# A sink logit kept as a 257th score column, and rotated queries in a shared scratch tile, in a two-layer decoder trunk

## The chip, the core and the metric

The kernel runs on one core of one Trainium2 chip. The metric is the device time of one execution in microseconds (us). Five instruction streams run side by side and meet through semaphores: PE (TensorE, matrix products; PEld is its weight load), DVE (VectorE), ACT (ScalarE), POOL (GpSimd) and SP (SyncE, which here only issues transfers). Each stream is executed strictly in its own order: an instruction that has to wait holds up everything behind it on its engine.

## The reference, cut to what matters

The program computes a two-layer decoder on 512 tokens of width 1024, in float32. The change touches the attention of layer 0: eight query heads in two groups that share one key and one value head each, a causal window of 128 tokens, and a learned logit per head (the sink) that enters the softmax's maximum and its denominator but has no value vector.

```python
def band_attention(q, k, v, max_dist, sink=None):
    s = jnp.einsum('bnqhgd,bnjhd->bnhgqj', qb, kk) * (hd ** -0.5)
    s = jnp.where(valid[None, :, None, None], s, -jnp.inf)
    m = jnp.max(s, axis=-1)
    m = jnp.maximum(m, sink_b)
    p = jnp.exp(s - m[..., None])
    l = jnp.sum(p, axis=-1)
    l = l + jnp.exp(sink_b - m)
    o = jnp.einsum('bnhgqj,bnjhd->bnqhgd', p.astype(v.dtype), vv)
    o = o / jnp.transpose(l, (0, 1, 4, 2, 3))[..., None]
    ...

def even_mixer(h, w_in, sinks, conv_w, conv_b, ln_g, ln_b, w_out, pos):
    proj = jnp.einsum('bsd,de->bse', h, w_in)
    q, k, v, glu = jnp.split(proj, [A_Q, A_Q + A_KV, A_Q + 2 * A_KV], axis=-1)
    q = rotary(q.reshape(B, S, A_HEADS, HEAD_DIM), pos)
    ...
    a, _ = band_attention(q, k, v, A_WINDOW - 1, sinks)
    c = g_a * jax.nn.sigmoid(g_b)
    c = causal_depthwise_conv(c, conv_w, conv_b)          # 31 taps
    c = jax.nn.silu(layer_norm(c, ln_g, ln_b))
    return jnp.einsum('bse,ed->bsd', jnp.concatenate([a, c], axis=-1), w_out)
```

After this mixer come a feed-forward block, a second mixer, a second feed-forward block and a last norm; none of their code changes.

## The kernel before, in words

Activations lie transposed, features on the 128 partitions and the 512 tokens along the row. Every large product is done as three matmuls, since both sides are split into a rounded part and its remainder: weights come from memory as 128x1024 blocks (`raw`), ACT makes the rounded half `w_hi` (L174), and DVE or POOL subtracts to make `w_lo` (L151). One 128x128 weight tile costs three matmuls of 512 columns (L201, L202, L203).

Layer 0's mixer runs, by the span of the profile, from about 25 us to about 200 us. PE's order there is written by hand: the string `C0["steps"]` lists the projections (`g0` to `g3` of the convolution's gate pairs, `v`, `k`, `q0` to `q3`) and the attention steps (`S0` to `S3` scores, `V0` to `V3` values, each for one pair of heads i and i + 4; "head 0" to "head 3" below are these pairs), and a class `Seq` weaves the small attention steps between the projections' weight tiles. On the other engines a scheduler sets the order when the program is built, from the dependencies, from priorities and from its own estimate of durations; so a change of one instruction there can move others.

What DVE does in this stage: the rotation of queries and keys (`rope`, L390 to L393), the split of the rotated queries (`qs`, L717), the masked minimum of the negated scores (L598, one per block of 128 queries and head: it writes the negated scaled scores to `Pm` and their row minimum with the negated sink to `nm`), the sink's terms (`es`, L605; `rl`, L614 and L615), the product with the reciprocal denominators that ends the values of a head pair (`on`, L430), and most taps of the convolution, each one instruction on 128x512 (L481 and L483, which adds into a bank of PSUM, and L484, which adds that to POOL's part `yc`). The convolution runs at a much lower priority (`LATER`). ACT does the exponentials (L610) with their row sums `l`, the sink's exponential (L612), the copies of transposed probabilities `pts` (L410), which PE's value products (L421) wait for, the copy `oh` (L363) of a finished head pair, and products `prod` (L478) of some taps, which POOL adds up (L479). `prod` has three buffers, so a fourth product waits for POOL's first add. POOL also makes `w_lo` here.

PE has two kinds of meeting point with this: L435 transposes `on`, so it waits for DVE's L430, and L407 transposes the probabilities `Pm` for the next head pair into a bank that ACT's L644 (`yn`, the convolution's transposed output) may still read.

## Time and profile before

| what | value |
|---|---|
| time of three runs | 1117.32, 1123.54, 1124.16 us; median 1123.54 us |
| the profiled execution | 1121.61 us, of which the span from first to last instruction is 1119.9 us |
| PE busy | 1071.8 us (96% of the span) |
| DVE busy | 693.8 us (62%) |
| ACT busy | 572.9 us (51%) |
| POOL busy | 232.8 us (21%) |
| granted TensorE clock, mean | 0.989 |

The shares are means over the whole span. The page's table of 40 slices (28 us each) shows that they hide a stage: DVE's digits are 9, 7 and 7 in slices 3 to 5 (56 to 140 us: 7, 7, 4 for ACT, 7, 5, 4 for POOL), and PE, which has 9 nearly everywhere, has 8 or 7 only in some places, of which slices 3 and 5 are two. Rows of the timeline give the start, the duration, engine, line, operation, what is written and read, how many instructions of a kind in a row, and in brackets the idle time ahead and what ended it.

### The profile page before, as it was taken

What the parts mean: (1) busy time and instruction counts of PE and PEld (TensorE: products, weight loads), DVE (VectorE), ACT (ScalarE), POOL (GpSimd) and SP (SyncE); (2) the same over time, 40 slices, a digit from 0 to 9 for tenths busy, and PEclk for the clock granted to TensorE, in tenths of its full rate; (3) what the DMA queues carried; (4) which work ended last, traced back from release to release, by engine and by line L of the source; (5) the groups of instructions that cost most, each with busy time, mean ns of one, the idle gap of its engine ahead of it and who ended that gap; (6) DMA issues with size and microseconds to landing.
All of it is one profiled execution on the core that took longest, in us unless ns stands there. A gap on an engine that the chain in (4) does not pass through costs nothing.

```text
span 1119.9 us, 13693 instructions
## 1 busy us (share of the span) xinstructions
PE 1071.8 (96%) x5118; PEld 887.8 (79%) x5118; DVE 693.8 (62%) x1059; ACT 572.9 (51%) x930; POOL 232.8 (21%) x210
## 2 busy tenths in 40 slices
PE   9988789989999999999999999999899999999997
PEld 7767677868788888888887888888688888888785
DVE  3889965777455655654748546666765646555543
ACT  6577756754435343543636654446544453535433
POOL 0789754201101010100014300001111010101002
PEclk9989999999999999999999999999999999999999
DMA  6221112977767677621432111239777676767122
GB/s 230 68 70 57 38 38 75 263 208 190 168 187 150 188 136 217 135 57 50 149 103 76 57 39 58 94 117 237 210 187 179 164 171 180 154 189 150 26 69 76
DMA packets 42803, 145.89 MB, mean 130 GB/s; under 512 B 4848, under 2 KB 5744, under 8 KB 42736
## 3 DMA queue, kind: packets, MB, share of 16 engines
q1 hardware_dynamic: 31072, 102.97, 27.0%
q0 software_dynamic: 11520, 41.95, 22.2%
q8 instruction: 40, 0.66, 0.2%
q14 instruction: 27, 0.22, 0.1%
q10 hardware_dynamic: 144, 0.09, 0.0%
HBM read 142.89 MB, written 2.10 MB: 129 GB/s over the span
## 4 chain that ended last, share of the span: by engine, by line
PE 75%; DVE 9%; DMA 4%; ACT 4%; issue 4%; POOL 3%; POOLq 0%; ACTq 0%; SPq 0%; DVEq 0%
PE bank L201 11%; PE bank L202 10%; PE bank L203 10%; PE bank L904 10%; PE bank L907 10%; PE bank L906 10%; DMA raw<-in_ws 4%; PE bank L262 2%; PE bank L264 2%; PE bank L263 2%; DVE bank L483 2%; PE bank L919 1%; PE bank L421 1%; ACT w2h L880 1%; POOL yc L479 1%
## 5 line engine op out<-in xcount | busy, mean ns | idle before, releaser
L151 DVE TENSOR_TENSOR w2l<-raw,w2h 128x1024 fp32r<-128x1024 f32 x140 | 171.4, 1225 | 206.0 <-ACT w2h L880 206.0
L880 ACT ACTIVATE w2h<-raw 128x1024 fp32r<-128x1024 f32 x140 | 148.0, 1058 | 208.8 <-PE bank L907 159.5
L174 ACT ACTIVATE w_hi<-raw 128x512 fp32r<-128x512 f32 x204 | 127.4, 628 | 180.5 <-PE bank L202 143.4
L870 POOL DMA_DIRECT2D raw<-in_ws x80 | 69.6, 870 | 557.7 <-DVE w2l L151 231.7
L151 DVE TENSOR_TENSOR w_lo<-raw,w_hi 128x512 fp32r<-128x512 f32 x164 | 115.6, 709 | 57.7 <-ACT w_hi L174 57.7
L907 PE MATMUL bank<-w2h,s 128*128 128x512 f32 x320 | 126.0, 394 | 4.3 <-DVE s L151 4.3
L904 PE MATMUL bank<-w2h,s 128*128 128x512 f32 x320 | 126.5, 395 | 2.5 <-ACT s L823 1.4
L906 PE MATMUL bank<-w2l,s 128*128 128x512 f32 x320 | 125.5, 392 | 0.0
L201 PE MATMUL bank<-xh,w_hi 128*128 128x512 f32 x272 | 111.4, 410 | 1.3 <-ACT w_hi L174 1.3
L203 PE MATMUL bank<-xh,w_lo 128*128 128x512 f32 x272 | 108.0, 397 | 0.0
L202 PE MATMUL bank<-xl,w_hi 128*128 128x512 f32 x272 | 107.9, 397 | 0.0
L201 PE MATMUL bank<-hh,w_hi 128*128 128x512 f32 x256 | 100.1, 391 | 1.1 <-DVE hl L151 1.1
L202 PE MATMUL bank<-hl,w_hi 128*128 128x512 f32 x256 | 100.0, 391 | 0.0
L203 PE MATMUL bank<-hh,w_lo 128*128 128x512 f32 x256 | 99.9, 390 | 0.0
L904 PE MATMUL bank<-w2h,xh 128*128 128x512 f32 x240 | 94.4, 393 | 0.0
L907 PE MATMUL bank<-w2h,xl 128*128 128x512 f32 x240 | 93.5, 389 | 0.0
L906 PE MATMUL bank<-w2l,xh 128*128 128x512 f32 x240 | 93.4, 389 | 0.0
L907 PEld LDWEIGHTS bank<-w2h,s 128*128 128x128 f32 x320 | 60.7, 190 | 17.9 <-DVE s L151 5.2
L904 PEld LDWEIGHTS bank<-w2h,s 128*128 128x128 f32 x320 | 60.6, 190 | 16.4 <-ACT s L823 2.3
L906 PEld LDWEIGHTS bank<-w2l,s 128*128 128x128 f32 x320 | 60.5, 189 | 12.4
L151 POOL TENSOR_TENSOR w_lo<-raw,w_hi 128x512 fp32r<-128x512 f32 x40 | 54.6, 1366 | 60.2 <-ACT w_hi L174 57.6
L479 POOL TENSOR_TENSOR yc<-yc,prod 128x512 f32<-128x512 f32 x44 | 60.7, 1381 | 10.5 <-ACT prod L478 9.0
(237 smaller groups left out, 2051.8 us busy)
## 6 DMA issues: line engine op xcount, KB each, us to landing
raw<-in_ws SPq DMA_DIRECT2D x181, 512.0 KB, 4.2
raw<-in_ws POOLq DMA_DIRECT2D x80, 512.0 KB, 5.7
h<-in_xT SPq DMA_DIRECT2D x8, 256.0 KB, 4.8
out_y<-xh SPq DMA_DIRECT2D x4, 256.0 KB, 2.0
out_y<-xl SPq DMA_DIRECT2D x4, 256.0 KB, 2.3
raw<-in_ws SPq DMA_DIRECT2D x2, 256.0 KB, 3.9
ropeC<-in_rope_c SPq DMA_DIRECT2D x2, 256.0 KB, 4.1
ropeS<-in_rope_s SPq DMA_DIRECT2D x2, 256.0 KB, 4.7
```

Of the source, the lines that this page charges most:

```text
L151: eng.tensor_tensor(out=out, in0=a, in1=b, op=ALU.subtract)
L174: A.activation(hi, src, AF.Copy)
L201: T.matmul(ps, hi, xh, start=start, stop=False)
L202: T.matmul(ps, hi, xl, start=False, stop=False)
L203: T.matmul(ps, lo, xh, start=False, stop=stop)
L262: T.matmul(ps[t], xh[:, c], hi, start=(k == 0), stop=False)
L479: G.tensor_add(yc[j], yc[j], p)
L870: nc.gpsimd.dma_start(t, ws[base + 8 * (g - 1) + 2 * BLOCK_OF[more] + q], accum_op=ALU.add)
L880: A.activation(hi, src, AF.Copy)
L904: T.matmul(ps[t], xh[:, c], wh[:, w], start=(start and j == 0), stop=False, skip_group_check=True)
L906: T.matmul(ps[t], xh[:, c], wl[:, w], start=False, stop=False, skip_group_check=True)
L907: T.matmul(ps[t], xl[:, c], wh[:, w], start=False, stop=(j == 3), skip_group_check=True)
```

## The change

The tile `Pm` (`[128, 8, 256]`) gets a 257th column. One ACT copy per head pair writes the negated sink logit there, for all eight rows of the pair; the exponential of L610 then runs over 257 columns (129 for the first block) and its row sum already holds the sink's term. The three instructions per head pair that made this term apart go: the sum `es` on DVE, its exponential on ACT, and the addition to `rl` on DVE. The scores' minimum (L598) writes and reads what it did, and the value products skip the new column.

The rotated queries, before in a tile `qT` of their own with three buffers, go to the scratch tile `gb` (two buffers, shared with the gate's sigmoid part and the rotated keys). The three early parts of the output projection, which had taken over `qT`'s buffers, go to `prod`'s.

```diff
@@ -459,7 +459,7 @@
         V.tensor_scalar(out=taps, in0=taps, scalar1=0.5, scalar2=None, op0=ALU.mult)
 
 
-        mp.tile([P, 8, 2 * P], F32, name="Pm", bufs=2)
+        mp.tile([P, 8, 2 * P + 1], F32, name="Pm", bufs=2)
         for b in range(2):
             mp.tile([P, S], F32R, name=f"qs{b}", bufs=2)
         yc = [mp.tile([P, S], F32, name=f"yc{j}") for j in range(4)]
@@ -574,8 +574,11 @@
             yield 0.0, C0["q"]
             while i >= 2 and ("V", i - 2) not in done:
                 yield 0.0, 0.3
-            qss = qTs[i][1]
-            Pm = mp.tile([P, 8, 2 * P], F32, name="Pm", bufs=2)
+            qss = qTs[i]
+
+            Pm = mp.tile([P, 8, 2 * P + 1], F32, name="Pm", bufs=2)
+            A.activation(Pm[:, :, 2 * P:].rearrange("p (n b) o -> p n (b o)", b=2),
+                         nsink[:, i:i + 5:4][:, None, :].to_broadcast([P, NQ, 2]), AF.Copy)
             nm = scr.tile([P, 8], F32, name="nm")
             l = scr.tile([P, 8], F32, name="l")
             for n2 in range(2):
@@ -596,23 +599,17 @@
                         c0 = P if n == 0 else 0
                         hd = i + 4 * b
                         V.tensor_tensor_reduce(
-                            out=Pm[:, u, c0:], in0=sb[b][:, n1 * 256 + c0:n1 * 256 + 256],
+                            out=Pm[:, u, c0:2 * P], in0=sb[b][:, n1 * 256 + c0:n1 * 256 + 256],
                             in1=mask0[:, c0:], scale=-0.125, scalar=nsink[:, hd:hd + 1],
                             op0=ALU.add, op1=ALU.min, accum_out=nm[:, u:u + 1])
                 if n2 == 0:
                     yield 0.9, C0["S"]
-            es = scr.tile([P, 8], F32, name="es")
-            V.tensor_tensor(out=es.rearrange("p (n b) -> p n b", b=2),
-                            in0=nm.rearrange("p (n b) -> p n b", b=2),
-                            in1=sinkb[:, i:i + 5:4][:, None, :].to_broadcast([P, NQ, 2]), op=ALU.add)
             for u in range(8):
                 c0 = P if u < 2 else 0
                 A.activation(Pm[:, u, c0:], Pm[:, u, c0:], AF.Exp, bias=nm[:, u:u + 1], scale=-1.0,
                              accum_out=l[:, u:u + 1])
-            A.activation(es, es, AF.Exp)
             rl = scr.tile([P, 8], F32, name="rl")
-            V.tensor_add(rl, l, es)
-            V.reciprocal(rl, rl)
+            V.reciprocal(rl, l)
             del qTs[i]
             pend[i] = Pm, rl, seq.t + 0.9 + C0["ST"]
             yield 0.9, 0.0
@@ -627,7 +624,7 @@
                 n, b = divmod(u, 2)
                 if n:
                     items.append((u, Pm[:, u, 0:P], n - 1, True, False))
-                items.append((u, Pm[:, u, P:], n, n == 0, True))
+                items.append((u, Pm[:, u, P:2 * P], n, n == 0, True))
             yield from pt_av(items, lambda u, blk: Vt[:, blk, 64 * (u % 2):64 * (u % 2) + 64], rl, i, (4, 7))
 
         def conv_norm():
@@ -706,11 +703,10 @@
             elif kind == "q":
                 ps = gemm_in(step)
                 seq.until(lambda: len(qTs) < 2)
-                qTs[i] = (mp.tile([P, S], F32, name="qT", bufs=3),
-                          [mp.tile([P, S], F32R, name=f"qs{b}", bufs=2) for b in range(2)])
+                qTs[i] = [mp.tile([P, S], F32R, name=f"qs{b}", bufs=2) for b in range(2)]
 
                 def after(i=i, ps=ps, step=step):
-                    qT, qss = qTs[i]
+                    qT, qss = scr.tile([P, S], F32, name="gb"), qTs[i]
                     rope(ps, qT, tabs, V if step in C0["rope_v"] else G)
                     for b in range(2):
                         A.activation(qss[b][rows[b]], qT[rows[b]], AF.Copy)
@@ -734,7 +730,7 @@
                 ps = bank(5)
                 for k in range(4):
                     acc3(ps, (oh[k], ol[k]), k == 0, k == 3)
-                early[i] = mp.tile([P, S], F32, name="qT", bufs=3)
+                early[i] = mp.tile([P, S], F32, name="prod", bufs=3)
                 A.activation(early[i], ps, AF.Copy)
             else:
                 if kind == "C":
```

The built program of the change has the same order on PE and on SP. On DVE, ACT and POOL instructions are moved. Lines from 580 on are shifted by three or four in the changed kernel: L601 there is L598 here, L609 is L610, L612 is L615, L640 and L641 are L643 and L644, L713 is L717.

On DVE, from the end of head 2's scores to `on` of head 2 (L430): `gb` and `cp` are the gate pair g3 and the convolution's input, `bank` the convolution's sum. Before:

```order
L483 SCALAR_TENSOR_TENSOR bank_914<-cp_126,cc,bank_914 128x512
L605 TENSOR_TENSOR es<-nm,sinkb 128x8
L614 TENSOR_TENSOR rl<-l,es 128x8
L615 RECIPROCAL rl<-rl 128x8
L498 TENSOR_TENSOR gb<-bank_1211,R 128x512
L484 TENSOR_TENSOR yc_138<-yc_138,bank_914 128x512
L502 SCALAR_TENSOR_TENSOR cp_127<-gb,ga 128x512
L481 TENSOR_SCALAR bank_1280<-cp_127,cc 128x512
L483 SCALAR_TENSOR_TENSOR bank_1280<-cp_127,cc,bank_1280 128x512 x10
L430 TENSOR_TENSOR on<-bank_1341,rl 128x512
```

In the changed kernel, at the same place:

```order
L483 SCALAR_TENSOR_TENSOR bank_912<-cp_126,cc,bank_912 128x512 x2
L612 RECIPROCAL rl<-l 128x8
L498 TENSOR_TENSOR gb<-bank_1206,R 128x512
L502 SCALAR_TENSOR_TENSOR cp_127<-gb,ga 128x512
L484 TENSOR_TENSOR yc_138<-yc_138,bank_912 128x512
L481 TENSOR_SCALAR bank_1271<-cp_127,cc 128x512
L483 SCALAR_TENSOR_TENSOR bank_1271<-cp_127,cc,bank_1271 128x512 x5
L430 TENSOR_TENSOR on<-bank_1332,rl 128x512
```

Five of the last convolution tile's taps have moved from ahead of `on` to behind it, and `cp` has moved ahead of `yc`.

On DVE, from the last scores of head 3 to `on` of head 3, which is the last of the four. Before:

```order
L483 SCALAR_TENSOR_TENSOR bank_1280<-cp_127,cc,bank_1280 128x512
L605 TENSOR_TENSOR es<-nm,sinkb 128x8
L483 SCALAR_TENSOR_TENSOR bank_1280<-cp_127,cc,bank_1280 128x512 x2
L614 TENSOR_TENSOR rl<-l,es 128x8
L615 RECIPROCAL rl<-rl 128x8
L484 TENSOR_TENSOR yc_139<-yc_139,bank_1280 128x512
L430 TENSOR_TENSOR on<-bank_1466,rl 128x512
```

(two more single L483 rows, alike to the first, stand ahead of L615 and of L484). In the changed kernel:

```order
L483 SCALAR_TENSOR_TENSOR bank_1271<-cp_127,cc,bank_1271 128x512 x3
L612 RECIPROCAL rl<-l 128x8
L483 SCALAR_TENSOR_TENSOR bank_1271<-cp_127,cc,bank_1271 128x512 x6
L430 TENSOR_TENSOR on<-bank_1454,rl 128x512
L483 SCALAR_TENSOR_TENSOR bank_1271<-cp_127,cc,bank_1271 128x512
L484 TENSOR_TENSOR yc_139<-yc_139,bank_1271 128x512
```

Nine taps stand ahead of `on` where five and the addition L484 stood.

On ACT, from head 2's first copy of transposed probabilities to its `oh`. Before:

```order
L410 ACTIVATE pts<-bank_1342 128x512
L475 ACTIVATE yc_139<-cp_127,cc 128x512
L478 ACTIVATE prod<-cp_127,cc 128x512 x3
L410 ACTIVATE pts<-bank_1349 128x512
L410 ACTIVATE pts<-bank_1364 128x512
L478 ACTIVATE prod<-cp_127,cc 128x512 x2
L410 ACTIVATE pts<-bank_1375 128x256
L174 ACTIVATE w_hi<-raw 128x512
L478 ACTIVATE prod<-cp_127,cc 128x512
L363 ACTIVATE oh_314<-bank_1394 128x512
```

(three more `prod` stand between the last `pts` and `w_hi`). In the changed kernel:

```order
L410 ACTIVATE pts<-bank_1333 128x512
L475 ACTIVATE yc_139<-cp_127,cc 128x512
L478 ACTIVATE prod<-cp_127,cc 128x512 x2
L410 ACTIVATE pts<-bank_1340 128x512
L478 ACTIVATE prod<-cp_127,cc 128x512
L410 ACTIVATE pts<-bank_1355 128x512
L410 ACTIVATE pts<-bank_1366 128x256
L174 ACTIVATE w_hi<-raw 128x512
L363 ACTIVATE oh_314<-bank_1385 128x512
```

(one more `prod` ahead of the last `pts`, two behind it, one behind `w_hi`). Two products, not three, stand ahead of the second `pts`, and seven, not nine, ahead of `oh`.

## Rows read from the trace of the kernel before

**Rows 1.** Busy time of each engine in one stretch of 20 us

```profile
core 0: us, PE busy (x) PEld busy (x) DVE busy (x) ACT busy (x) POOL busy (x), PEclk, DMA share, GB/s
100.00:120.00 20.00, 13.75 (x87) 11.71 (x86) 19.68 (x34) 12.63 (x25) 18.30 (x13) 0.95 0.17 54
```

**Rows 2.** Timeline of PE: the waits from 87 us to 155 us

```profile
87.49 0.63 PE L435 MATMUL bank<-ident,on 128*128 128x128 f32 x4 [0.89 <-DVE on L430]
...
105.97 1.09 PE L407 MATMUL bank<-ident,Pm 128*128 128x128 f32 x8 [2.78 <-ACT yn L644]
...
117.00 0.66 PE L435 MATMUL bank<-ident,on 128*128 128x128 f32 x4 [3.47 <-DVE on L430]
...
129.95 0.47 PE L201 MATMUL bank<-oh,w_hi 128*128 128x512 f32 x1 [1.31 <-DVE gb L498]
...
135.01 1.10 PE L421 MATMUL bank<-Vt,pts 128*128 128x64 f32 x8 [1.28 <-ACT pts L410]
...
140.54 0.66 PE L435 MATMUL bank<-ident,on 128*128 128x128 f32 x4 [1.48 <-DVE on L430]
...
154.10 0.66 PE L435 MATMUL bank<-ident,on 128*128 128x128 f32 x4 [1.24 <-DVE on L430]
```

**Rows 3.** Timeline of DVE: the sink's additions

```profile
80.34 1.12 DVE L605 TENSOR_TENSOR es<-nm,sinkb 128x8 f32<-128x8 f32 x1
...
94.98 1.26 DVE L605 TENSOR_TENSOR es<-nm,sinkb 128x8 f32<-128x8 f32 x1
...
99.43 1.11 DVE L614 TENSOR_TENSOR rl<-l,es 128x8 f32<-128x8 f32 x1
...
126.61 1.15 DVE L605 TENSOR_TENSOR es<-nm,sinkb 128x8 f32<-128x8 f32 x1
128.04 0.96 DVE L614 TENSOR_TENSOR rl<-l,es 128x8 f32<-128x8 f32 x1 [0.28 <-ACT es L612]
...
149.39 0.17 DVE L605 TENSOR_TENSOR es<-nm,sinkb 128x8 f32<-128x8 f32 x1
```

**Rows 4.** Timeline of POOL around the first and the last of these

```profile
76.69 4.75 POOL L479 TENSOR_TENSOR yc<-yc,prod 128x512 f32<-128x512 f32 x3
...
156.66 1.29 POOL L151 TENSOR_TENSOR w_lo<-raw,w_hi 128x512 fp32r<-128x512 f32 x1 [10.02 <-ACT w_hi L174]
```

**Rows 5.** DVE's groups by line from 60 us to 160 us: busy, mean ns

```profile
L483 DVE SCALAR_TENSOR_TENSOR bank<-cp,cc,bank 128x512 f32<-128x512 f32 x52 | 39.0, 750 | 0.6
L598 DVE CUSTOM_DVE_ANT_0 Pm<-bank,mask,nsink 128x256 f32<-128x256 f32 x24 | 10.6, 479 | 0.7 <-PE bank L591 0.7
...
L392 DVE TENSOR_TENSOR rb<-rb,ropeS 128x512 f32<-128x512 f32 x3 | 3.2, 1078 | 0.0
```

**Rows 6.** Timeline of ACT: ahead of two instructions

```profile
17.98 0.63 ACT L527 ACTIVATE prod<-h 128x512 f32<-128x512 f32 x1 [1.50 <-PE bank L529]
...
81.50 0.21 ACT L612 ACTIVATE es<-es 128x8 f32<-128x8 f32 x1 [1.11 <-DVE es L605]
```

**Rows 7.** Timeline of PE: last matmuls of two projections

```profile
96.91 0.39 PE L203 MATMUL bank<-xh,w_lo 128*128 128x512 f32 x1
...
128.25 0.39 PE L203 MATMUL bank<-xh,w_lo 128*128 128x512 f32 x1
```

**Rows 8.** Timeline of DVE: the negated sink, and what reads those projections

```profile
16.74 0.17 DVE L453 TENSOR_SCALAR nsink<-sinkb 128x8 f32<-128x8 f32 x1
...
97.54 0.68 DVE L390 TENSOR_TENSOR ra<-bank,ropeC 128x512 f32<-128x512 f32 x1
...
129.16 0.64 DVE L498 TENSOR_TENSOR gb<-bank,R 128x512 f32<-128x512 f32 x1
```

**Rows 9.** Timeline of PE after the longest wait: matmuls of one kind

```profile
118.69 0.63 PE L201 MATMUL bank<-xh,w_hi 128*128 128x512 f32 x1
...
121.25 0.51 PE L201 MATMUL bank<-xh,w_hi 128*128 128x512 f32 x1
...
122.06 0.39 PE L201 MATMUL bank<-xh,w_hi 128*128 128x512 f32 x1
```

## Prediction

> **What bounds the kernel now.** I read the page's table of slices first, to find the stages in which PE, the engine with 96% of the span, is not full; then the busy times by stretch, PE's timeline for the waits inside that stage, and last the timelines of the engines that PE waits for. The change lies in layer 0's mixer, and its attention runs from about 69 to 155 us. In the stretch from 100 to 120 us [rows 1] DVE is busy 19.68 of 20 us and PE 13.75: there the end is set by DVE. The waits of PE [rows 2] say where the two meet: four times at L435, which needs DVE's `on` of a head pair (0.89, 3.47, 1.48 and 1.24 us of idle time), once at L407, which needs ACT's `yn` (2.78), once for DVE's `gb` (1.31) and once for ACT's `pts` (1.28). Behind 154.10 us PE has no further wait of this kind before the feed-forward block; so what the last `on` comes earlier, the whole rest of the program comes earlier. That row is the one to follow.

> **What the change removes.** Per head pair two DVE additions on 128x8 and one ACT exponential on 128x8; four of each. The additions are tiny, but in [rows 3] they take 1.12, 1.26, 1.11, 1.15 and 0.96 us; only where POOL stands idle, at 149.39, is it 0.17. (POOL waits 10.02 us ahead of 156.66 [rows 4], so it has been idle since 146.6.) The first one ends at 80.34 + 1.12 = 81.46, and POOL's run of three additions ends at 76.69 + 4.75 = 81.44 [rows 3, 4]: the small addition waits until POOL has finished. [...]

> Now pair by pair, along DVE's order.

> *Head 0.* The addition `es` goes, 1.1 us off DVE ahead of `on`. ACT too had waited for it, 1.11 us ahead of L612 at 81.50 [rows 6], and the `pts` behind L612 come earlier, so PE is ready for `on` earlier as well. The wait at 87.49 was 0.89 us; with PE ahead by half a microsecond the whole 1.1 us arrives. Lead of PE: 1.1.

> *Head 1.* The `es` at 94.98 brings nothing more: shortly behind it DVE takes up the projection of head 2's queries at 97.54 [rows 8], whose last matmul starts at 96.91 and takes 0.39 [rows 7], so DVE is there at most 0.2 us after PE, and PE leads by only 1.1. The `rl` addition (1.11) lies behind this point, ahead of the rotation that `qs` on ACT, `yn` behind it, and `on` of head 1 depend on. But the next DVE instruction is L392, again with two SBUF inputs, and the three of its kind take 1.078 on average [rows 5] against 0.68 of L390, alike in size, with one input in PSUM [rows 8]; right behind `rl` it had nothing left to wait for, now it may. I take 1.11 - 0.4 + 0.1 (the reciprocal is earlier) = 0.8. One tap fewer stands ahead of `on` (six L483 where there were seven): 0.75 [rows 5]. The lead at 117.00 is 1.1 + 0.8 + 0.75 = 2.65. L407's wait at 105.97 shrinks by more (`yn` also changes places with a `w_hi`), but PE then waits longer for `on`.

> *Head 2.* `es`, its wait and `rl` (1.15 + 0.28 + 0.96) lie ahead of `gb` at 129.16, and `gb` needs PE's last matmul, 128.25 + 0.39 = 128.64 [rows 3, 7, 8]. So of 2.4 us only some 0.45 is to be had. Lead at 129.95: 3.1. Behind it things are moved: on ACT one `prod` fewer precedes the second `pts`, on DVE `cp` no longer stands behind `yc`. The 1.28 us wait at 135.01 then goes all but 0.1: lead 4.3. Five taps leave the way to `on` (5 x 0.75 = 3.75), more than the 1.48 of wait at 140.54; I count 1.2, as PE comes to the limit itself. Lead 5.5. `oh` of ACT, two products earlier, keeps pace with it.

> *Head 3.* Here the taps come back: nine L483 (6.75 us) stand ahead of the last `on`, where five (3.75), the addition L484 (counted 0.7, like a tap) and the two short sink additions (0.3) stood. That is 2.0 us later against the last scores. Lead at 154.10: 5.5 - 2.0 = 3.5. PE's wait there becomes 1.24 + 2.0 = 3.2 us.

> *The clock.* A wait of that length has occurred: 3.47 us ahead of 117.00. [...] 3.2 is nearer to 3.47, so I count the fall: 6 x 0.16 = 1.0, and 0.3 for scores ahead of them: 1.3. Lead that remains: 2.2 us.

> **What the change adds, at no cost.** The copy of the sink into `Pm`: four ACT instructions on 128x8, each like the exponential that goes (0.21 [rows 6]). The first two stand in front of a product that waits 1.50 us for PE at 17.98; they need `nsink`, ready at 16.74 + 0.17 = 16.91 [rows 6, 8], and 0.4 us of work fits; were it late, PE's first sums of squares would be held by as much. The other two stand behind `pts` copies, long ahead of the scores that fill the tile. One column more per exponential is lost in a duration of half a microsecond. `gb` in two buffers: each rotated query is read by `qs` before the next but one user writes, in DVE's own order, so nothing new waits. The early output parts take `prod` buffers at about 158 us, and POOL is through with its last product at 146.6 [rows 4]. SP's queue is the same; the feed-forward block's first weight buffers lie over other tiles of the mixer, all read long before they are asked for.

> **The sum.** The profiled execution took 1121.61 us. Together with the three timed runs (1117.32, 1123.54, 1124.16) the middle of four is 1122.6, 1 us under their median of 1123.54. I set the forecast against 1122.6: 1122.6 - 2.2 = 1120.4 us.

> **Rivals.**
> *The wait is handed on.* POOL does no less, so a two-input DVE instruction behind the removed one may wait in its place. By the rows each addition then gives back only its bare 0.17, some 1.3 us for all eight, and head 3's extra 2.0 and the clock's 1.3 eat it up: 1122.6 to 1124.2. For it: L392 behind `rl`, and its mean of 1.078. Against: behind each `es` and behind three of the `rl` comes an instruction with one input in PSUM, a tap, `yc` or `gb`. [...]
> *DVE passes it all on.* If no new idle time appears on DVE and the clock doesn't fall, the last `on` moves by everything that leaves its front: 3.5 (three `es`) + 2.4 (four `rl`) + 0.3 + 0.7 + 0.75 - that is 7.6, and 1115.0. Against it: DVE would have to overtake PE's projections at 97.54 and 129.16, which it can't; with those two losses (1.2 and 2.0) it is 4.4, and without a fall of the clock 1118.2.
> *Odd rows make `Pm` slow; slower.* Rows of `Pm` now start 1028 bytes apart. If L598's writes took twice as long, 24 x 0.479 + 8 x 0.35 = 14.3 us would come onto the engine that sets the end: 1122.6 - 3.5 + 14.3 = 1133.4. From 0.07 us per instruction (2.2 / 32) it cancels the lead. Against it: the 52 taps read `cp` at offsets that grow by 4 bytes, and take 0.750 on average [rows 5], with an aligned output.
> *The moved order decides, the other way.* If the wait for `pts` stays or ACT's products, paced by POOL, hold `oh`, the lead at 140.54 is 2.5 instead of 5.5, and the last `on` comes 0.5 us ahead of before: with the clock's fall 1123.4.

> **How the numbers follow.** The forecast case (1118 to 1122) gets 0.50; the wait handed on and the moved order together (1122 to 1125) 0.30; DVE's full gain (1114.5 to 1118) 0.13; slow `Pm` 0.05; the rest 0.02. The range runs from 1114.5 to 1126, with the runs' own spread at the upper end. One per cent, 11 us, is about what a measurement of this kernel can tell from no change; nearly all cases lie within it: faster 0.05, same 0.92, slower 0.03 (half of the slow `Pm`, the other half stays below 1135).

> **What the changed kernel's profile would show.** DVE without any 128x8 addition in the stage, the reciprocals at about 0.2; L598 and L483 at their old means; PE's waits at L435 of 0.9, 3.5, almost none, and 3 us or more for head 3, followed by matmuls at 0.43; the last L435 at about 150.6 instead of 154.10, with everything behind it shifted alike. I am wrong if `es`'s time turns up again in L392, L393 or `qs` (L717), if the last L435 comes at 153 us or later, or if a stage behind 155 us swallows the lead, above all the first weight blocks of the feed-forward part.

## The result and the profile after

The changed kernel takes 1134.50 us (median of four runs, 1132.2 to 1136.19), the kernel before 1121.71 us beside it (four runs, 1117.32 to 1124.16): ratio 1.0113, 95% interval 1.0085 to 1.0141. It is slower by 1.1%, some 13 us, where 2 us less were forecast; the time lies outside the range. Measured again beside other kernels it was 1132.60 us, ratio 1.0087 (1.0064 to 1.0111).

The first view to read is the page after: span, busy times, and the groups of large matmuls (the columns are busy time, mean ns of one, idle time ahead). L900, L902 and L903 are L904, L906 and L907 of the kernel before.

```profile
span 1133.7 us, 13694 instructions
PE 1087.9 (96%) x5118; PEld 890.8 (79%) x5118; DVE 690.4 (61%) x1051; ACT 573.1 (51%) x930; POOL 233.2 (21%) x210
...
L903 PE MATMUL bank<-w2h,s 128*128 128x512 f32 x320 | 126.3, 395 | 3.8 <-DVE s L151 3.8
L201 PE MATMUL bank<-xh,w_hi 128*128 128x512 f32 x272 | 111.2, 409 | 1.1 <-ACT w_hi L174 1.1
L201 PE MATMUL bank<-hh,w_hi 128*128 128x512 f32 x256 | 101.9, 398 | 1.2 <-DVE hl L151 1.2
L900 PE MATMUL bank<-w2h,xh 128*128 128x512 f32 x240 | 95.7, 399 | 0.0
```

The same groups on the page of before:

```profile
L907 PE MATMUL bank<-w2h,s 128*128 128x512 f32 x320 | 126.0, 394 | 4.3 <-DVE s L151 4.3
L201 PE MATMUL bank<-xh,w_hi 128*128 128x512 f32 x272 | 111.4, 410 | 1.3 <-ACT w_hi L174 1.3
L201 PE MATMUL bank<-hh,w_hi 128*128 128x512 f32 x256 | 100.1, 391 | 1.1 <-DVE hl L151 1.1
L904 PE MATMUL bank<-w2h,xh 128*128 128x512 f32 x240 | 94.4, 393 | 0.0
```

PE is busy 16.1 us longer with the same 5118 matmuls, in a program whose feed-forward code did not change. Its idle time didn't grow: 1133.7 - 1087.9 = 45.8 us against 48.1. And it is not every matmul: `hh,w_hi` and `w2h,xh` take 6 to 7 ns more, `w2h,s` and `xh,w_hi` do not. (In these names the first tile is the moving one, read in 512 columns, the second the stationary one of 128x128.)

How regular this is shows the timeline of PE in the second feed-forward block. These are the first starts of two blocks of 48 matmuls, in before and then in after:

```profile
1001.65 0.39 PE L904 MATMUL bank<-w2h,xh 128*128 128x512 f32 x1
...
1012.53 0.39 PE L904 MATMUL bank<-w2h,xh 128*128 128x512 f32 x1
```

```profile
1014.38 0.40 PE L900 MATMUL bank<-w2h,xh 128*128 128x512 f32 x1
...
1025.58 0.40 PE L900 MATMUL bank<-w2h,xh 128*128 128x512 f32 x1
```

The 48 matmuls from the first row to the second take 10.88 us before, 226.67 ns from start to start (called their pitch below), and 11.20 us after, 233.33 ns; PE doesn't wait in between, and the granted clock is 1.00 in both (1000 to 1013 us before, 1014 to 1026 after). Where `w2h,s` and `w2l,s` alternate, in the first feed-forward block, 71 matmuls take 16.10 us in both kernels (472.38 to 488.48 us before, 478.64 to 494.74 after).

The mixer, which the prediction is about, went much as it said. PE's waits there, to be read against [rows 2] (L407 waits for L641 now, L435 is the same line):

```profile
85.36 0.63 PE L435 MATMUL bank<-ident,on 128*128 128x128 f32 x4 [0.57 <-DVE on L430]
...
102.00 1.09 PE L407 MATMUL bank<-ident,Pm 128*128 128x128 f32 x8 [0.94 <-ACT yn L641]
...
113.17 1.12 PE L435 MATMUL bank<-ident,on 128*128 128x128 f32 x4 [3.59 <-DVE on L430]
...
126.91 0.47 PE L201 MATMUL bank<-oh,w_hi 128*128 128x512 f32 x1 [0.88 <-DVE gb L498]
...
131.38 1.10 PE L421 MATMUL bank<-Vt,pts 128*128 128x64 f32 x8 [0.68 <-ACT pts L410]
...
135.65 0.66 PE L435 MATMUL bank<-ident,on 128*128 128x128 f32 x4 [0.17 <-DVE on L430]
...
151.10 1.12 PE L435 MATMUL bank<-ident,on 128*128 128x128 f32 x4 [3.61 <-DVE on L430]
```

The lead grows to 140.54 - 135.65 = 4.89 us and is 3.00 us at the last `on`. It does not last: by 160 us, behind that wait, 0.36 us of it are left, as the part on the clock below shows. Two lines of ACT's timeline show what follows, before and then after: the weights of the first feed-forward block.

```profile
206.75 1.99 ACT L880 ACTIVATE w2h<-raw 128x1024 fp32r<-128x1024 f32 x2
...
215.00 1.06 ACT L880 ACTIVATE w2h<-raw 128x1024 fp32r<-128x1024 f32 x1 [4.69 <-DMA raw<-in_ws]
```

```profile
206.41 1.99 ACT L876 ACTIVATE w2h<-raw 128x1024 fp32r<-128x1024 f32 x2
...
216.74 1.06 ACT L876 ACTIVATE w2h<-raw 128x1024 fp32r<-128x1024 f32 x1 [6.77 <-DMA raw<-in_ws]
```

At 206 us 0.34 us of lead are left, and then ACT waits for a block of weights that landed 1.74 us later than before; DVE and PE stand behind it. At 241.69 us (before 239.49) the lag is 2.2 us, and the remaining 13.8 - 2.2 = 11.6 us of the spans' difference gather until the end, in the slower pitch: some 5.6 us to 550 us, 1.3 to 750 us and 4.7 behind it.

### The profile page after: what moved, and what is told of

The parts are those of the page before. It is cut to its first block, busy times and chain, and to the rows that moved or that the text cites. A ratio compares the mean times of both kernels' runs of the same rounds, so it can differ in the third digit from the quotient of the medians.

```text
span 1133.7 us, 13694 instructions
## 1 busy us (share of the span) xinstructions
PE 1087.9 (96%) x5118; PEld 890.8 (79%) x5118; DVE 690.4 (61%) x1051; ACT 573.1 (51%) x930; POOL 233.2 (21%) x210
## 4 chain that ended last, share of the span: by engine, by line
PE 77%; DVE 8%; DMA 4%; issue 4%; ACT 4%; POOL 2%; SPq 0%; POOLq 0%; ACTq 0%
PE bank L201 11%; PE bank L202 11%; PE bank L203 11%; PE bank L900 10%; PE bank L903 10%; PE bank L902 10%; DMA raw<-in_ws 4%; PE bank L262 2%; PE bank L264 2%; PE bank L263 2%; DVE bank L483 2%; PE bank L915 1%; PE bank L421 1%; ACT w2h L876 1%; DVE w2l L151 1%
## 5 line engine op out<-in xcount | busy, mean ns | idle before, releaser
L900 PE MATMUL bank<-w2h,s 128*128 128x512 f32 x320 | 127.0, 397 | 4.2 <-ACT s L819 3.2
L903 PE MATMUL bank<-w2h,s 128*128 128x512 f32 x320 | 126.3, 395 | 3.8 <-DVE s L151 3.8
L902 PE MATMUL bank<-w2l,s 128*128 128x512 f32 x320 | 126.0, 394 | 0.0
L900 PE MATMUL bank<-w2h,xh 128*128 128x512 f32 x240 | 95.7, 399 | 0.0
L902 PE MATMUL bank<-w2l,xh 128*128 128x512 f32 x240 | 94.8, 395 | 0.0
L903 PE MATMUL bank<-w2h,xl 128*128 128x512 f32 x240 | 94.8, 395 | 0.0
L900 PEld LDWEIGHTS bank<-w2h,s 128*128 128x128 f32 x320 | 60.7, 190 | 18.4 <-ACT s L819 4.0
L903 PEld LDWEIGHTS bank<-w2h,s 128*128 128x128 f32 x320 | 60.7, 190 | 17.9 <-DVE s L151 5.0
L902 PEld LDWEIGHTS bank<-w2l,s 128*128 128x128 f32 x320 | 60.8, 190 | 12.8
L930 DVE TENSOR_TENSOR h<-h,bank 128x512 f32<-128x512 f32 x69 | 47.1, 685 | 27.2 <-PE bank L203 27.2
```

What stands on the lines that cost most here:

```text
L900: T.matmul(ps[t], xh[:, c], wh[:, w], start=(start and j == 0), stop=False, skip_group_check=True)
L902: T.matmul(ps[t], xh[:, c], wl[:, w], start=False, stop=False, skip_group_check=True)
L903: T.matmul(ps[t], xl[:, c], wh[:, w], start=False, stop=(j == 3), skip_group_check=True)
L930: V.tensor_add(h[n], h[n], ps)
```

## What the difference could be

The two programs differ in one more thing than the diff says. `es` was a tile of the pool `scr`, two buffers of 32 bytes; without it, everything that is laid out behind `scr` begins 64 bytes lower in each partition, and that is the feed-forward blocks and layer 1's mixer (in layer 0's mixer the 64 bytes that `Pm`'s two buffers gain make up for it; `oh0` there stays at 174496):

| tile (bytes from the partition's start) | before | after |
|---|---|---|
| `xh0`, `w_hi`, `w_lo` | 34144, 79200, 87392 | the same |
| `w2h`, `hh`, `s1` (feed-forward) | 111456, 168800, 185184 | 111392, 168736, 185120 |
| `oh0`, `st` (layer 1) | 159584, 186208 | 159520, 186144 |

These are the addresses in the two built programs. In before all these lie a multiple of 512 bytes from one another. In after, `w2h` and `xh`, or `hh` and `w_hi`, no longer do; `w2h` and `s`, or `xh` and `w_hi`, still do. That is the line between slow and unchanged groups. Taking, for each matmul of 512 columns and the stationary tile loaded for the next one, the address of the stationary operand minus that of the moving one, modulo 256, the mean times from start to start (those of 200 to 300 ns) in after are: 0 apart 228.1 ns (1,813 of them, those next to slow ones included), 64 apart 233.2 (1,745), 192 apart 229.5 (350). This is theory A, places. Its rivals: B, a lower level of PE that begins after the two long waits or the wait at 231 us; C, that the 257th column or the scratch tile brings the time itself.

## Experiments

**The changed kernel with the old places.**

```diff
+            scr.tile([P, 8], F32, name="es")
             rl = scr.tile([P, 8], F32, name="rl")
             V.reciprocal(rl, l)
```

> The changed kernel, with the two 32-byte buffers of `es` still reserved in `scr` and not used, so that every tile of the feed-forward blocks and of layer 1's mixer lies again at the address that it has in the kernel before (in the changed kernel it lies 64 bytes lower). Theory A (places): 1,745 matmuls of the changed kernel, those whose moving tile lies 64 bytes lower and that overlap the load of a stationary tile that stayed, start 233.2 ns apart instead of 227.1; 1,745 x 6.1 ns = 10.7 us, and some 1 us from other pairs. With the old places these pitches are 227 again and the time is 1134.5 - 11.7 = 1122.8, range 1120 to 1125. Theory B (state): PE's slower pitch is a level that the chip takes after the second 3.6 us wait in the mixer and the wait of 2.38 us at the start of the feed-forward block; the waits stay, so 1133 to 1136. Theory C (the 257th column or the scratch tile themselves cost the 11 us): 1133 to 1136 as well.

Measured: 1120.49 us (median of 12 runs), before 1121.35 us; ratio 1.0012 (0.9989 to 1.0035). One reserved tile that nobody uses takes the whole loss back. C falls, since the column and the scratch tile are still there, and B with the two waits of 3.6 us, which are too. (The third wait of B, at the start of the feed-forward block, is only 0.63 us here; that it doesn't set the pitch either is seen in the next experiment, where it is 0.29 us and the pitch slow, and in the one on the feed-forward blocks alone, where it is 1.66 us and the pitch there is fast.) The profiled execution is with 1130.94 us the longest of the twelve (PE is already 5.9 us late at 69 us, and later still at 242), so its pitch is to be read and not its span: the same 48 matmuls take 10.88 us.

```profile
1012.31 0.39 PE L901 MATMUL bank<-w2h,xh 128*128 128x512 f32 x1
...
1023.19 0.39 PE L901 MATMUL bank<-w2h,xh 128*128 128x512 f32 x1
```

**The kernel before with the new places.**

```diff
-            es = scr.tile([P, 8], F32, name="es")
+            es = mp.tile([P, 8], F32, name="es", bufs=2)
```

> The kernel before, with the same instructions in the same order; only the tile `es` is taken from the pool mix0 instead of scr, so that every tile behind scr lies 64 bytes lower, as in the changed kernel. Theory A (places): the feed-forward blocks and layer 1's mixer take the changed kernel's pitch of 233.2 ns for the same 1,745 matmuls, and the time is 1121.7 + 11.7 = 1133.4, range 1131 to 1136. Theories B (a state after the mixer's waits) and C (the 257th column or the scratch tile): nothing of theirs is in it, so 1121.7, range 1117 to 1125.

Measured: 1133.78 us, ratio 1.0109 (1.0087 to 1.0131), with the instructions of before in their old order on all engines. The 48 matmuls take 11.20 us, as in the changed kernel:

```profile
1014.17 0.40 PE L904 MATMUL bank<-w2h,xh 128*128 128x512 f32 x1
...
1025.37 0.40 PE L904 MATMUL bank<-w2h,xh 128*128 128x512 f32 x1
```

Together the two are the proof: the places alone make the loss, and without it the change has no measurable effect.

**The kernel before, 64, 128 and 256 bytes higher.** Each reserves one more tile that isn't used; `[P, 16]` and `[P, 32]` instead of `[P, 8]` give the larger distances.

```diff
             es = scr.tile([P, 8], F32, name="es")
+            scr.tile([P, 8], F32, name="pad")
```

> The kernel before with 64 bytes more in scr, not used, so that every tile behind them lies 64 bytes higher. Theory A in two readings. Signed: in the changed kernel, matmuls whose stationary tile lies 64 bytes above the moving one (modulo 512) start 233.2 ns apart, those where it lies 64 below 229.1. Here the two kinds change places: 1,745 x 2.0 + 190 x 6 = 4.6 us, so 1126, range 1124 to 1128. Unsigned (only the distance modulo 128 counts): as with 64 bytes less, 1133, range 1131 to 1136. Theories B and C: 1121.7, range 1117 to 1125.

> The kernel before with only half of the third experiment's distance, two buffers of 16 bytes (rounded up to what the pool gives, 32 bytes each, or 64 in all, so that it repeats the third experiment if the pool rounds). Theory A: if the places come out 64 bytes higher, the third experiment's 1125.0 again, range 1122 to 1128; if 32 bytes higher, between 1121.4 and 1125.0. Rival (the third experiment's 1125.0 was scatter): 1121.4.

> The kernel before with everything behind scr 128 bytes higher. Theory A, distance counted modulo 512: the few pairs of the earlier runs that lie 128 apart took 232.3 to 232.9 ns; 1,745 pairs with 232.6 instead of 227.1 give 9.6 us and the 190 of the other sign up to 1.1: 1132, range 1129 to 1134. Theory A', distance counted modulo 128: nothing changes, 1121.4, range 1118 to 1124.

> The kernel before with everything behind scr 256 bytes higher. Theory A with a period of 512 or more: 2 to 6 ns for 1,745 pairs, 3.5 to 11 us, 1125 to 1133. With a period of 256: nothing changes, 1121.4, range 1118 to 1124.

Measured: 64 bytes 1125.01 us, ratio 1.0039 (1.0016 to 1.0061); what was meant as 32 bytes is 64 as well, since the pool rounds each buffer up, and repeats it with 1.0036 (1.0016 to 1.0056); 128 bytes 1134.01 us, 1.0104 (1.0068 to 1.0140); 256 bytes 1122.80 us against 1123.49, 1.0005 (0.9980 to 1.0029). The 48 matmuls in these three:

```profile
1007.79 0.39 PE L905 MATMUL bank<-w2h,xh 128*128 128x512 f32 x1
...
1018.78 0.39 PE L905 MATMUL bank<-w2h,xh 128*128 128x512 f32 x1
```

```profile
1012.07 0.39 PE L905 MATMUL bank<-w2h,xh 128*128 128x512 f32 x1
...
1023.23 0.39 PE L905 MATMUL bank<-w2h,xh 128*128 128x512 f32 x1
```

```profile
1001.86 0.39 PE L905 MATMUL bank<-w2h,xh 128*128 128x512 f32 x1
...
1012.74 0.39 PE L905 MATMUL bank<-w2h,xh 128*128 128x512 f32 x1
```

That is 10.99, 11.16 and 10.88 us. With the 11.20 of the changed kernel it makes a table for one and the same 48 matmuls:

| stationary minus moving address, modulo 256 | ns from start to start | kernel |
|---|---|---|
| 0 | 226.7 | before; 256 bytes higher |
| 64 | 233.3 | after; `es` elsewhere |
| 128 | 232.5 | 128 bytes higher |
| 192 | 229.0 | 64 bytes higher |

So the signed reading held (the rival that 64 bytes either way cost the same, 1133, did not), a distance of 256 bytes is like none (226.7 ns) and one of 128 is not (232.5), and it is the distance of the two operands that counts: with 64 bytes more, pairs that were both moved keep 227.0 ns (929 of them).

**Only the feed-forward blocks at the old places.**

```diff
+            fp.tile([P, 16], F32, name="pad")
             homes = [fp.tile([P, 1024], F32R, name=x, bufs=3) for x in ("w2h", "w2l")]
```

> The changed kernel with 64 bytes, not used, at the head of the pool ffn alone: the tiles of the two feed-forward blocks lie again where they lay before, those of layer 1's mixer stay 64 bytes lower. Theory A (places): of the 11.7 us, the changed kernel's trace puts 5.3 into the first feed-forward block, 4.9 into the second and 2.3 into layer 1's mixer between them; so 10 us go: 1124.5, range 1122 to 1127. In the trace the pitches of the feed-forward blocks are 227, and 249 of layer 1's mixer stay at 233. Rival (a level of PE that begins at one moment and lasts to the end): all or nothing, 1134 or 1121.

> The changed kernel itself, on the same chip as the two above, so that they are compared with it directly. Theory A: 1.0113 of the kernel before, as in the first measurement, within 1.008 to 1.014.

Measured: 1122.43 us against 1132.60 of the changed kernel on the same chip, 10.2 us less, as its trace had put into these blocks; against before 1.0008 (0.9987 to 1.0030). The 48 matmuls are back at 10.88 us (1001.96 to 1012.84), and in layer 1's mixer 194 pairs stay at 233.2 ns. A level of PE that begins at a moment could not end and begin again with the tile.

**One half alone, and the mixer in step.** The first is the scratch half of the diff alone (no `qT`; the sink as before). The second is the first experiment with 384 unused bytes more behind `Pm`, which brings the mixer's output projection in step too.

> The kernel before with the second half of the change alone: rotated queries in `gb`, the early output parts in `prod`, no tile `qT`; the sink is added as before and `es` stays. All tiles of the feed-forward blocks and of layer 1 keep their addresses. Theory A (places): no slow pitch, and what is left is the order of the taps, which waits 2 us at the last `on` and gains as much ahead of it: 1121.7, range 1118 to 1125. Theory C' (the scratch half brings the slow pitch, by tiles used again sooner or by the order of the taps): 1130 or more. Theory B (the second long wait sets the pitch): 1133 if the wait ahead of the last `on` is 3 us or more.

> The changed kernel with `es` still reserved in scr (as in the first experiment) and 384 bytes more, not used, behind `Pm` in layer 0's mixer, so that the query, output and weight tiles of that mixer too lie at a multiple of 512 bytes from `xh` and the weights. Theory A (places): the 160 pitches of layer 0's output projection that lay 128 bytes apart and took 232.9 ns (before: 64 bytes apart, 170 of 229.3) become 227: 160 x 5.9 = 0.9 us off the first experiment's 1120.5, so 1119.6, range 1117 to 1122; every group of pitches at 227. Rival (the mixer's matmuls are held by something else than the places): 1120.5, the pitches of the output projection stay above 229.

Measured: the scratch half 1121.63 us against 1121.35, ratio 1.0004 (0.9993 to 1.0016): nothing. Its wait ahead of the last `on` is 1.24 us, as in [rows 2], so the moved taps come with the column half. With the mixer in step 1123.01 us against 1123.49, ratio 1.0004 (0.9983 to 1.0024): all 3,902 pairs of its trace lie at 227.2 ns, but a gain of 0.9 us can't be told from none.

**Fewer taps ahead of the last `on`.**

```diff
-    taps=(8, 15, 15, 10),
+    taps=(8, 15, 15, 12),
```

> The fifth experiment's kernel (all tiles in step) with 12 instead of 10 as the last number of the taps: two more of the last convolution tile's taps are ACT products that POOL adds up, so that seven taps instead of nine stand on DVE ahead of the last `on`. Theory M (the second long wait is what the mixer still loses): the wait of 3.6 us ahead of the last L435 becomes 2.1, the clock doesn't fall behind it, and 1.5 + 1.6 = 3.1 us come off: 0.997 of the kernel before or a little more, 1119 to 1121 where before takes 1122 to 1123. Rival 1 (ACT's two products delay the exponentials and `pts`): the wait keeps its length, no change against the fifth experiment, ratio 0.999 to 1.002. Rival 2 (the feed-forward block starts on `s` of ACT and DVE and on its weights, and takes the lead back at 230 us): the last L435 is earlier by 1.5 or more, the time is not.

Measured: 1121.88 us against 1122.81, ratio 1.0001 (0.9983 to 1.0019). The wait did shrink, by more than expected, but the clock fell all the same, earlier. Here are the last wait in PE's timeline, and the stretch from 140 to 160 us (its length, the busy times of PE, PEld, DVE, ACT and POOL, then the granted clock):

```profile
151.82 1.12 PE L435 MATMUL bank<-ident,on 128*128 128x128 f32 x4 [0.78 <-DVE on L430]
```

```profile
140.00:160.00 20.00, 16.83 (x80) 14.56 (x79) 11.58 (x26) 9.31 (x22) 9.49 (x8) 0.74 0.07 27
```

In the fifth experiment's kernel the wait is 3.60 us and the clock of the stretch 0.83. Theory M is refuted as it was put: what PE saved at the wait it lost in slower matmuls ahead of it (eight value products from 146.35 us take 1.80 us, where eight from 144.89 us take 1.09 in the changed kernel) and behind it (from 153.16 to 155.72 us the output projection's start 0.43 us apart). No version was found that is faster than the kernel before.

## Why the prediction was wrong

**The step that failed** is "What the change adds, at no cost". It weighed each added instruction and each buffer that is shared, and noted that SP's queue stays the same and where the first weight buffers lie, but it put the space of the tile that goes, `es`, at nothing, and gave no reason. Its 64 bytes moved all tiles of the feed-forward blocks and of layer 1's mixer out of step with `xh` and the weights, and some 1,900 matmuls pay 2 to 6.6 ns each: 11.6 us of the 13. None of the rivals contained it: "odd rows make `Pm` slow" came near the time (1133.4) for a reason that isn't there.

**"So what the last `on` comes earlier, the whole rest of the program comes earlier"** failed as well, by 2 us. The lead was 3.00 us at 151.10, and 0.34 at 206 us, since the clock took more than forecast (below); then a weight block landed 1.74 us later. The prediction named the first weight blocks as what would make it wrong, but gave that no price. This loss is one trace's, and it isn't shown that the change causes it: in the second trace of the changed kernel the block is there at 215.47 us, only 0.47 later than before, and PE is as late at 241 us. The kernel before with the new places loses the same 2 us without the change's instructions, at a wait for ACT's `ga`. These are the same matmul in before, in after and in that kernel:

```profile
239.49 0.50 PE L904 MATMUL bank<-w2h,s 128*128 128x512 f32 x1 [0.39 <-ACT ga L978]
```

```profile
241.69 0.50 PE L900 MATMUL bank<-w2h,s 128*128 128x512 f32 x1 [0.58 <-ACT ga L974]
```

```profile
242.02 0.80 PE L904 MATMUL bank<-w2h,s 128*128 128x512 f32 x1 [1.99 <-ACT ga L978]
```

What sets this stage's end stays open. Of the forecast 2.2 us nothing is shown: with the old places the medians are 0.9, 0.5 and 0.9 us below before's (the first, the all-in-step and the taps kernel), but the ratios are 1.0012, 1.0004 and 1.0001, and a gain can't be told from none.

**The steps in the mixer, one by one.** Leads at the meeting points, forecast and measured (by [rows 2] and the rows above): 1.1 and 2.13 at head 0, 2.65 and 3.83 at head 1, 3.1 and 3.04 at the projection, 4.3 and 3.63 at `pts`, 5.5 and 4.89 at head 2, 3.5 and 3.00 at the last `on`, with a wait of 3.61 where 3.2 was forecast. The first two are not the change's alone. The traces agree at 69 us, but at 75 us, ahead of the first `es`, after already leads by 1.09 us: the granted clock from 60 to 80 us is 0.91 where it was 0.83. The kernel before with the new places, which has the old instructions, has 0.91 there too, and is 1.12 us ahead at head 0:

```profile
86.37 0.63 PE L435 MATMUL bank<-ident,on 128*128 128x128 f32 x4 [0.88 <-DVE on L430]
```

So the change's own share is some 1.0 at head 0 and 2.7 at head 1, close to the forecast; the rest is scatter of the clock. The taps kernel, whose clock there is 0.83 as in before, leads by 0.86, 2.56 and 2.97 us at head 0, head 1 and the projection, where after's extra lead is gone as well. Of the nine taps ahead of the last `on`, three stand ahead of the reciprocal and six behind it:

```profile
143.37 2.33 DVE L483 SCALAR_TENSOR_TENSOR bank<-cp,cc,bank 128x512 f32<-128x512 f32 x3
145.61 0.20 DVE L612 RECIPROCAL rl<-l 128x8 f32<-128x8 f32 x1
145.74 4.71 DVE L483 SCALAR_TENSOR_TENSOR bank<-cp,cc,bank 128x512 f32<-128x512 f32 x6
150.36 0.68 DVE L430 TENSOR_TENSOR on<-bank,rl 128x512 f32<-128x512 f32 x1
```

**The clock** fell, as forecast, but cost more than 1.3 us. The granted clock of the stretch from 140 to 160 us is 0.83 (before 1.00), and the output projection's first matmuls behind the wait start 0.43 us apart:

```profile
151.87 0.78 PE L201 MATMUL bank<-oh,w_hi 128*128 128x512 f32 x1
...
156.71 0.40 PE L203 MATMUL bank<-oh,w_lo 128*128 128x512 f32 x1
```

Eleven matmuls take 4.84 us instead of 11 x 0.227 = 2.50, so 2.3 us of the 3.0 go here at once, and 2.6 by 160 us: twice the 1.3 that the prediction counted. The 1.3 was an estimate from the wait of 3.47 us before, behind which the granted clock fell: six matmuls of [rows 9] start 0.43 us apart there and the next three 0.27, and four scores from 117.89 to 118.69 us 0.20, where those from 74.75 us start 0.12 apart. That fall was half as long: the clock is 0.50 from 118.1 to 121.5 us before, and from 149.9 to 156.7 us in the changed kernel.

**The additions' time came back in part.** `es` and `rl` took 3.7 + 2.4 = 6.1 us of DVE from 60 to 160 us. Each of the five long ones ends 0.02 to 0.03 us behind an instruction of POOL (which end at 81.44, 96.22, 100.52, 127.74 and 128.99 us); the three others take 0.16 to 0.17 us. In the same stretch of the changed kernel other instructions with two inputs in SBUF are longer: `rb` of L392 3.7 us where it took 3.2 [rows 5], `qs` 6.4 where it took 6.0, L393 3.4 (3.2), L502 2.6 (2.3). By line, engine and shape (busy time, mean ns):

```profile
L713 DVE TENSOR_TENSOR qs<-gb,qs 64x512 fp32r<-64x512 f32 x6 | 6.4, 1059 | 0.2
L392 DVE TENSOR_TENSOR rb<-rb,ropeS 128x512 f32<-128x512 f32 x3 | 3.7, 1230 | 0.0
L393 DVE TENSOR_TENSOR gb<-ra,rb 128x512 f32<-128x512 f32 x3 | 3.4, 1118 | 0.0
```

That is at most 1.4 of 6.1 us handed on (that these wait for POOL in the additions' place is not shown); the rival that all is handed on is refuted by the leads above. `Pm`'s odd rows cost nothing that shows, as said (478 ns where it was 479, and 750 for the taps in both):

```profile
L483 DVE SCALAR_TENSOR_TENSOR bank<-cp,cc,bank 128x512 f32<-128x512 f32 x52 | 39.0, 750 | 0.8
L601 DVE CUSTOM_DVE_ANT_0 Pm<-bank,mask,nsink 128x256 f32<-128x256 f32 x24 | 10.6, 478 | 0.7 <-PE bank L594 0.7
```

**Two readings.** The page of before gives DVE 8, 9 and 9 in slices 3 to 5 (ACT 7, 7 and 7, POOL 8, 9 and 7), not the digits told ahead of the prediction; DVE is fuller there than was said, and the argument, which goes by the waits, doesn't change.

```profile
DVE  3889965777455655654748546666765646555543
```

The rival that the wait is handed on would by its own terms (1.3 back, 2.0 and 1.3 lost) end at 1124.6, not 1124.2.

The sink's copies were covered: the first two wait 0.46 us for `nsink`, and the product behind them starts at 17.97 us, which before started at 17.98 [rows 6].

## What to carry to other kernels

When a change adds, drops or resizes a tile, compare the addresses of all tiles behind it before counting instructions, and keep the operands of the large matmuls in step (here a multiple of 256 bytes apart: 226.7 ns per matmul, against 229.0 to 233.3); an unused tile that holds the place cost no time that could be measured (ratio 1.0012, 0.9989 to 1.0035). If PE's busy time grows with the same count of matmuls, split the groups by operand: which pairs became slower says more than any wait. And a lead gained in one stage is worth only what the next stages let through: here the slower matmuls behind the last wait took 2.6 us of 3.0.
